# Weighted values of attention: one product of 128 columns for each block of keys in place of two of 64

## The chip, the core and the metric

The kernel runs on one core of a Trainium2 chip. TensorE (PE in the profile) multiplies matrices: it loads a stationary operand of up to 128 x 128 (weight loads, PEld in the profile) and moves a second operand through it into PSUM. VectorE (DVE), ScalarE (ACT) and GpSimd (POOL) work element by element, and SyncE (SP) issues most of the transfers. The metric is the device time of one execution in microseconds (us), lower is better.

## The reference

One layer of an encoder over 1024 tokens of width 1024: a SwiGLU feed-forward half step, then attention and an RWKV-7 scan side by side, an output projection, and a second feed-forward half step. Inputs and result are float32. The part that the change touches is the attention, 8 heads of 64 features with three banded patterns, each a softmax over the keys of its band, mixed by their denominators:

```python
DILATED_PATTERNS = ((128, 1), (512, 4), (2048, 16))

def _attention_group(za, cos, sin, out_g):
    ...
    for window, dilation in DILATED_PATTERNS:
        o, l = _dilated_attention(q, k, v, window, dilation)
        outs.append(o)
        lses.append(l)
    wts = jax.nn.softmax(jnp.stack(lses, axis=0), axis=0)
    o = jnp.sum(wts[..., None] * jnp.stack(outs, axis=0), axis=0)
    o = o * lax.rsqrt(jnp.mean(o * o, axis=-1, keepdims=True) + NORM_EPS)
    return o.reshape(B, S, ATT_WIDTH) * out_g

def _dilated_attention(q, k, v, window, dilation):
    ...
    s = jnp.where(valid, s, -jnp.inf)
    m = jnp.max(s, axis=-1, keepdims=True)
    p = jnp.exp(s - m)
    den = jnp.sum(p, axis=-1, keepdims=True)
    o = jnp.einsum('bhrnqk,bhrnkd->bhrnqd', p, vb.astype(jnp.float32)) / den
```

The product `p` by `v` in the last line is the one that is changed, for the first two patterns.

## The kernel before

The layer is worked off in stages: the first feed-forward half (about 0 to 640 us of the profiled execution), the projections (to 928), the attention with part of the RWKV projections beside it (928 to 1182), preparation and scan of the RWKV group with the output projection (to about 1600), the second feed-forward half.

In the attention the tokens are in 8 blocks of 128. The first two patterns are taken together in `near`: for a block of 128 queries, only the keys of at most 5 blocks count (two before, two after), 34 pairs of blocks for each head. `scores(t)` multiplies queries and keys of block `t` (L713, L714, in split single-pass float32), adds the band's bias and takes the maximum on VectorE (L715), and the exponential on ScalarE (L718). `turn(t)` transposes the 128 x 128 pieces of the exponentials on TensorE (L727), so that keys lie on partitions, and copies them out of PSUM (L728). `values(t)` multiplies them by the values and adds up over the key blocks in one PSUM tile `po` of 128 queries x 8 blocks x 64 features (L734). These run as a pipeline: in step `t` stand `scores(t)`, `turn(t - 1)` and `values(t - 2)`. When a head is done, `po` is scaled on VectorE (L758).

The third pattern, of stride 16, is worked in `far` for the next head between these steps (scores L655, transposes L666, values L673, on 64 x 64 parts of the array). After each head comes one stream of the RWKV projection (L523, 48 products of 512 columns; L599 and L609 belong to it). A scheduler orders all of it: it interleaves the products of L523 with those of the attention, so that each engine's list of instructions is fixed before the run, and TensorE works its list off in order. In the products of L655 and L673 and, before the change, of L734, the stationary operand has 64 columns and the result goes to partitions 0 to 63 or 64 to 127.

Of the kernel before, what the change touches and what calls it, by code (L numbers as in the profile page):

```python
# [31 lines left out]
def _ap(src, off, pat):  # L32
    return bass.AP(tensor=src.tensor, offset=src.offset + off, ap=pat)
# [130 lines left out]
class _Kernel:  # L164
# [529 lines left out]
    def near(self, psum, p, h, sq, kh, kl, v, far, between):  # L694

        nc, V, A, G, T = self.nc, self.nc.vector, self.nc.scalar, self.nc.gpsimd, self.nc.tensor
        hs = slice(h % 2 * 64, h % 2 * 64 + 64)
        nm, d = (p.tile([128, NT], F32, name=n, tag=n) for n in ("nm", "dn"))
        M = p.tile([128, 4 * NT], F32, name="M", tag="M")[:, :NT]
        cc = p.tile([128, 2, NT], F32, name="cc", tag="cc")  # L700
        po = psum.tile([128, NT, 64], F32, name="po", tag="o", bufs=1)
        S_, E_ = {}, {}
        keys = lambda t: (max(0, t - 2), min(NT, t + 3))

        def scores(t):
            k0, k1 = keys(t)
            n, qs = (k1 - k0) * 128, slice(t * 128, (t + 1) * 128)
            bias = self.bias12[:, (k0 - t + 2) * 128:(k0 - t + 2) * 128 + n]
            s = S_[t] = p.tile([128, 640], F32, name="sb", tag="sb")
            for c in range(0, n, 512):  # L710
                e = min(n, c + 512)
                ps = psum.tile([128, 512], F32, name="s12", tag="s", bufs=2)
                T.matmul(ps[:, :e - c], sq[:, qs], kh[:, k0 * 128 + c:k0 * 128 + e], start=True, stop=False)  # L713
                T.matmul(ps[:, :e - c], sq[:, qs], kl[:, k0 * 128 + c:k0 * 128 + e], start=False, stop=True)  # L714
                V.tensor_tensor_reduce(out=s[:, c:e], in0=ps[:, :e - c], in1=bias[:, c:e], scale=-1.0,  # L715
                                       scalar=nm[:, t:t + 1] if c else 3e38, op0=OP.add, op1=OP.min,
                                       accum_out=nm[:, t:t + 1])
            A.activation(s[:, :n], s[:, :n], AF.Exp, bias=nm[:, t:t + 1], scale=-1.0, accum_out=d[:, t:t + 1])  # L718

        def turn(t):  # L720
            n, s = (keys(t)[1] - keys(t)[0]) * 128, S_.pop(t)
            et = E_[t] = p.tile([128, 640], F32, name="e12", tag="e12")
            for c in range(0, n, 512):
                w = min(n - c, 512)
                pt = psum.tile([128, 512], F32, name="pt12", tag="t", bufs=2)
                for i in range(w // 128):
                    T.transpose(pt[:, i * 128:(i + 1) * 128], s[:, c + i * 128:c + (i + 1) * 128], self.ident)  # L727
                (V.tensor_copy if (t % 2 and not c) else A.copy)(et[:, c:c + w], pt[:, :w])  # L728

        def values(t):  # L730
            (k0, k1), et = keys(t), E_.pop(t)
            for i in range(k1 - k0):
                for c in range(0, 128, 64):
                    T.matmul(po[c:c + 64, t, :], et[:, i * 128 + c:i * 128 + c + 64], v[:, k0 + i, hs], start=(i == 0),  # L734
                             stop=(i == k1 - k0 - 1))

        for step in range(NT + 2):
            if step < NT:
                between(step)
                scores(step)  # L740
            if 1 <= step < NT + 1:
                turn(step - 1)
            if step >= 2:
                values(step - 2)
        f = far
        o = h % 2 * 64
        fd, fm, c12, c3 = f[:, :, o], f[:, :, 65], cc[:, 0], cc[:, 1]
        V.scalar_tensor_tensor(M, fm, -1.0, nm, op0=OP.mult, op1=OP.min)
        V.tensor_tensor(c12, M, nm, op=OP.subtract)
        V.tensor_tensor(c3, fm, M, op=OP.add)  # L750
        A.activation(cc, cc, AF.Exp)
        V.tensor_tensor(d, d, c12, op=OP.mult)
        V.tensor_tensor(M, fd, c3, op=OP.mult)
        V.tensor_tensor(d, d, M, op=OP.add)
        V.reciprocal(d, d)
        V.tensor_tensor(cc, cc, d[:, None, :].to_broadcast([128, 2, NT]), op=OP.mult)
        y = p.tile([128, NT, 64], F32, name="ya", tag="ya", bufs=1)
        V.tensor_tensor(y, po, c12[:, :, None].to_broadcast([128, NT, 64]), op=OP.mult)  # L758
        f3 = f[:, :, 1 - h % 2:65 - h % 2]
        G.tensor_tensor(f3, f3, c3[:, :, None].to_broadcast([128, NT, 64]), op=OP.mult)  # L760
        G.tensor_tensor(y, y, f3, op=OP.add)
        G.tensor_tensor(f3, y, y, op=OP.mult)
        V.tensor_reduce(out=self.ss_a[:, :, h], in_=f3, op=OP.add, axis=AX.X)
        self.nc.scalar.dma_start(_ap(self.ya_d, h * 64, [[512, 128], [128 * 512, NT], [1, 64]]), y)
# [710 lines left out]
```

## Time and profile before

| | |
|---|---|
| Median of 3 runs | 2297.95 us (2295.15 to 2307.57) |
| Profiled execution | span 2299.0 us; nothing is recorded around it |
| TensorE busy | 2198.8 us, 96% of the span |
| TensorE weight loads | 1781.8 us, 77% |
| VectorE, ScalarE, GpSimd busy | 77%, 45%, 23% |
| Products of L734 | 1088 records between 928.4 and 1179.2 us |

A record is one instruction on the chip. Matmuls are pipelined, so the length of one record (0.22 us for L734) is longer than the distance from its start to the start of the next, the pitch. In the views of groups, a line names the source line, the engine, the operation, the output and inputs, the stationary operand (128*64: 128 partitions, 64 columns) and the moving one (128x64), the number of records; then busy time in us and mean length in ns, then idle time of the engine just before them and what ended it. A row in order of time gives start and length in us.

### The profile page before, as it was taken

How to read it: one execution, taken by the hardware profiler on the slowest of the kernel's cores; microseconds unless marked ns; L12 is line 12 of the kernel's file. 1: busy time of each engine (PE TensorE's matmuls, PEld its weight loads, DVE VectorE, ACT ScalarE, POOL GpSimd, SP SyncE). 2: the span in 40 equal slices, each digit the busy share in tenths (PEclk: the TensorE clock that was granted, in tenths of full speed). 3: DMA queues.
4: the chain of work that ended last, by engine and by line, in shares of the span. 5: the costliest groups of instructions: out<-in, count | busy, mean ns of one | idle time of the engine just before them, and what ended most of it. 6: DMA issues, size and time to landing. Idle time of an engine off the chain costs nothing. (4 is left out here: it accounts for less than half of the span.)

```text
span 2299.0 us, 41391 instructions
## 1 busy us (share of the span) xinstructions
PE 2198.8 (96%) x15556; PEld 1781.8 (77%) x15556; DVE 1767.3 (77%) x2893; ACT 1023.6 (45%) x1925; POOL 537.0 (23%) x673
## 2 busy tenths in 40 slices
PE   7999999999999998999998899999799999999998
PEld 5788888878877676777776777776678888888887
DVE  7999999865676254677679678747999999997566
ACT  5322323354567411666654644455442323335453
POOL 2354443410000011222221111122024444441000
PEclk9999999999999999999999799999899999999999
DMA  5354545486662513654467746357445454548665
GB/s 151 124 183 151 170 147 173 164 266 193 193 225 78 212 72 105 186 147 144 131 178 184 211 136 167 107 173 257 155 135 174 150 174 151 170 152 282 194 194 187
DMA packets 346700, 387.74 MB, mean 169 GB/s; under 512 B 73474, under 2 KB 249346, under 8 KB 346500
## 3 DMA queue, kind: packets, MB, share of 16 engines
q1 hardware_dynamic: 294928, 271.71, 39.2%
q0 software_dynamic: 31216, 100.73, 11.6%
q10 hardware_dynamic: 20356, 12.66, 1.8%
q8 instruction: 122, 2.00, 0.4%
q14 instruction: 78, 0.64, 0.1%
HBM read 258.06 MB, written 126.94 MB: 167 GB/s over the span
## 5 line engine op out<-in xcount | busy, mean ns | idle before, releaser
L81 PE MATMUL gu<-xh,wh 128*128 128x512 f32 x704 | 277.3, 394 | 4.6 <-ACT wh L186 4.5
L186 ACT ACTIVATE wh<-raw 128x512 fp32r<-128x512 f32 (+1 forms) x273 | 168.3, 627 | 252.3 <-PE gu L81 95.7
L81 PE MATMUL gu<-xl,wh 128*128 128x512 f32 x704 | 276.0, 392 | 0.0
L81 PE MATMUL gu<-xh,wl 128*128 128x512 f32 x704 | 275.9, 392 | 0.0
L187 DVE TENSOR_TENSOR wl<-raw,wh 128x512 fp32r<-128x512 f32 (+1 forms) x273 | 270.4, 994 | 3.7 <-ACT wh L186 3.0
L421 PE MATMUL pd<-gl,gwh 128*128 128x512 f32 x616 | 240.6, 391 | 2.6 <-DVE gl L187 2.6
L421 PE MATMUL pd<-gh,gwh 128*128 128x512 f32 x616 | 239.8, 390 | 0.6 <-DVE row L86 0.6
L421 PE MATMUL pd<-gh,gwl 128*128 128x512 f32 x616 | 240.1, 390 | 0.2 <-DVE gwl L187 0.2
L86 DVE TENSOR_TENSOR row<-gu,row 128x512 f32<-128x512 f32 x308 | 206.6, 683 | 25.8 <-PE gu L81 23.5
L187 DVE TENSOR_TENSOR gwl<-graw,gwh 128x512 fp32r<-128x512 f32 (+2 forms) x187 | 118.8, 643 | 124.0 <-ACT gwh L186 122.3
L116 POOL DMA_DIRECT2D d_hid<-row x154 | 84.7, 551 | 546.0 <-DVE row L114 524.2
L186 ACT ACTIVATE gwh<-graw 128x512 fp32r<-128x512 f32 (+2 forms) x187 | 103.1, 554 | 187.2 <-PE pd L421 151.3
L81 PEld LDWEIGHTS gu<-xh,wh 128*128 128x128 f32 x704 | 133.4, 190 | 33.6 <-ACT wh L186 5.6
L81 PEld LDWEIGHTS gu<-xh,wl 128*128 128x128 f32 x704 | 133.2, 189 | 27.7 <-DVE wl L187 0.2
L81 PEld LDWEIGHTS gu<-xl,wh 128*128 128x128 f32 x704 | 133.3, 189 | 27.4
L421 PEld LDWEIGHTS pd<-gl,gwh 128*128 128x128 f32 x616 | 115.7, 188 | 27.8 <-DVE gl L187 3.9
L421 PEld LDWEIGHTS pd<-gh,gwh 128*128 128x128 f32 x616 | 115.6, 188 | 25.5 <-DVE row L86 1.0
L421 PEld LDWEIGHTS pd<-gh,gwl 128*128 128x128 f32 x616 | 115.7, 188 | 24.1 <-DVE gwl L187 0.6
L187 DVE TENSOR_TENSOR gl<-raw,gh 128x512 fp32r<-128x512 f32 x160 | 114.7, 728 | 22.9 <-ACT gh L186 22.6
L94 ACT ACTIVATE row<-row 128x512 f32<-128x512 f32 x44 | 27.8, 633 | 212.0 <-DVE row L86 212.0
L145 POOL TENSOR_TENSOR ws<-ws 128x512 f32<-128x512 f32 x88 | 114.6, 1303 | 1.2
L186 ACT ACTIVATE gh<-raw 128x512 fp32r<-128x512 f32 x160 | 98.1, 622 | 35.5 <-DMA raw<-in_ffn_w_down_dram 22.8
(364 smaller groups left out, 5238.2 us busy)
## 6 DMA issues: line engine op xcount, KB each, us to landing
d_hid<-row POOLq DMA_DIRECT2D x154, 256.0 KB, 2.5
graw<-d_hid SPq DMA_DIRECT2D x132, 256.0 KB, 2.9
raw<-in_ffn_w_gate_dram SPq DMA_DIRECT2D x88, 256.0 KB, 3.1
raw<-in_ffn_w_up_dram SPq DMA_DIRECT2D x88, 256.0 KB, 3.6
ws<-in_ffn_w_down_dram SPq DMA_DIRECT2D x88, 256.0 KB, 4.1
d_ws<-ws POOLq DMA_DIRECT2D x88, 256.0 KB, 2.3
raw<-d_ws SPq DMA_DIRECT2D x88, 256.0 KB, 2.8
raw<-in_ffn_w_down_dram SPq DMA_DIRECT2D x66, 256.0 KB, 3.6
```

Source lines behind the costliest of these rows:

```text
L81: self.K.nc.tensor.matmul(ps, a[:, k, :], b[:, k, :], start=(k == 0 and i == 0), stop=(k == 3 and i == 2))
L86: add = lambda o, x: V.tensor_tensor(o, ps, x, op=OP.add)
L94: A.activation(y[:, 0], y[:, 0], AF.Silu)
L116: put = lambda n, y: G.dma_start(self.hid[n - 1, j // 2], y)
L145: G.tensor_tensor(o, a, b, op=OP.subtract)
L186: self.nc.scalar.activation(h, src, AF.Copy)
L187: (eng or self.nc.vector).tensor_tensor(l, src, h, op=OP.subtract)
L421: T.matmul(ps[x], a[:, ts], b, start=(m == 0 and k == 0), stop=(m == NM - 1 and k == 2))
```

## The change

The two products of a key block, which each took 64 of the 128 queries as the stationary operand and wrote one half of the partitions, become one product with all 128 queries as the stationary operand. The moving operand, the 64 columns of the head's values, stays the same. The result is the same sum.

```diff
         def values(t):
             (k0, k1), et = keys(t), E_.pop(t)
             for i in range(k1 - k0):
-                for c in range(0, 128, 64):
-                    T.matmul(po[c:c + 64, t, :], et[:, i * 128 + c:i * 128 + c + 64], v[:, k0 + i, hs], start=(i == 0),
-                             stop=(i == k1 - k0 - 1))
+                T.matmul(po[:, t, :], et[:, i * 128:i * 128 + 128], v[:, k0 + i, hs], start=(i == 0),
+                         stop=(i == k1 - k0 - 1))
```

The line of the product moves from L734 to L733, and later lines by one. TensorE's list, at the end of the second head (query blocks 4 to 7), before; `pt` are transposes, `po` the products that are changed, `zr` the projections beside:

```order
L727 MATMUL pt_9355<-ident,sb 128x128 x4
L727 MATMUL pt_9361<-ident,sb 128x128
L734 MATMUL po<-vn,e_9328 64x64 x10
L523 MATMUL zr<-xh_5416,zh 128x512
L727 MATMUL pt_9381<-ident,sb 128x128 x4
L734 MATMUL po<-vn,e_9354 64x64 x10
L523 MATMUL zr<-xl_5417,zh 128x512
L523 MATMUL zr<-xh_5416,zl 128x512
```

The same place in the changed kernel:

```order
L733 MATMUL po<-vn,e_9214 128x64 x5
L714 MATMUL s_9251<-kl,sq 128x384
L523 MATMUL zr<-xl_5417,zh 128x512
L727 MATMUL pt_9236<-ident,sb 128x128 x4
L727 MATMUL pt_9242<-ident,sb 128x128
L523 MATMUL zr<-xh_5416,zl 128x512
L523 MATMUL zr<-xh_5416,zh 128x512
L523 MATMUL zr<-xl_5417,zh 128x512
L523 MATMUL zr<-xh_5416,zl 128x512
L727 MATMUL pt_9257<-ident,sb 128x128 x4
L733 MATMUL po<-vn,e_9235 128x64 x5
```

Ten products of 64 rows of output are five of 128; they stand in as many runs (74) as before, and the first block's run has moved ahead of the second score product of block 6. TensorE's list, where the far pattern's values (L673) come directly behind such a run, in the changed kernel:

```order
L727 MATMUL pt_9166<-ident,sb 128x128 x4
L727 MATMUL pt_9172<-ident,sb 128x128
L733 MATMUL po<-vn,e_9134 128x64 x5
L673 MATMUL po3t<-v_9048,e_9117 64x65 x8
L713 MATMUL s_9209<-kh,sq 128x128
```

There are five such places in the list before and five in the list of the changed kernel. On the other engines the instructions are the same in number and kind; their order differs in places, in the attention and in the scan behind it.

## Prediction

> **What bounds the kernel now.** I read the page first, then the busy time by stages, then what TensorE waits for in the stage of the change, then the instructions of that stage in order of time.
>
> ```profile
> span 2299.0 us, 41391 instructions
> 640.00:928.00 288.00, 274.83 (x1245) 207.98 (x1244) 147.39 (x208) 129.41 (x222) 21.09 (x31) 0.98 0.40 136
> 928.00:1182.00 254.00, 248.41 (x2454) 198.59 (x2453) 186.58 (x456) 163.69 (x377) 65.98 (x72) 0.99 0.49 147
> 1182.00:1520.00 338.00, 304.88 (x5319) 253.65 (x5319) 249.37 (x722) 164.09 (x296) 51.98 (x96) 0.88 0.63 174
> ```
>
> The last three lines are stages: length, then the busy time of PE, its weight loads, DVE, ACT and POOL, the granted clock, DMA. From 928 to 1182 us runs the banded attention, the only stage that the change touches. TensorE is busy 248.41 of its 254 us; DVE has 67 us free and ACT 90. What TensorE waits for there, by the view of waits:
>
> ```profile
> PE s L713 <- DVE nm L715: 2.2, 3, 1.0
> PE pt L727 <- ACT sb L718: 1.8, 3, 0.7
> PE s L713 <- DVE sb L659: 0.7, 1, 0.7
> PE po3s L673 <- DVE nm L715: 0.3, 1, 0.3
> PE pt L727 <- ACT e L728: 0.2, 1, 0.2
> ```
>
> That is 5.2 us in 254. The rest of the stage is TensorE's own order of work, so what the products of L734 gain or lose there moves the stage's end. What follows the stage stands behind it on the same queue: the first piece that the chain of waits holds is
>
> ```profile
> 1187.47 5.37 DMA d_v<-us
> ```
>
> a store of what the last products of L523 gave, and those stand behind the attention on TensorE. So I pass a change of the stage on one for one.
>
> **What the products of L734 cost now.** The view of the line:
>
> ```profile
> L734 PEld LDWEIGHTS po<-vn,e x1088: 132/138/228, 928.4 to 1179.1; 128*64 128x64 f32 x182
> L734 PE MATMUL po<-vn,e x1088: 221/222/369, 928.4 to 1179.2; 128*64 128x64 f32 x182
> ```
>
> The program has 8 heads x 34 key blocks x 2 halves = 544 products; the trace has 1088 records, so a product of this type (f32) is two loads and two passes. Their length (222 ns) is mostly pipeline; what counts is the pitch from start to start. Two places, in order of time (start, length, then the instruction), and the lengths of one record of L727 (least, median, most):
>
> ```profile
> 1004.32 0.73 PE L727 MATMUL pt<-ident,sb 128*128 128x128 f32 x5
> 1004.98 0.80 PE L734 MATMUL po<-vn,e 128*64 128x64 f32 x20
> 1005.71 0.50 PE L713 MATMUL s<-kh,sq 128*128 128x512 f32 x1
> 1006.05 0.39 PE L714 MATMUL s<-kl,sq 128*128 128x512 f32 x1
> ...
> 1021.25 0.40 PE L523 MATMUL zr<-xh,zl 128*128 128x512 f32 x1
> 1021.57 0.57 PE L734 MATMUL po<-vn,e 128*64 128x64 f32 x12
> 1022.07 0.50 PE L523 MATMUL zr<-xh,zh 128*128 128x512 f32 x1
> 1022.40 0.39 PE L523 MATMUL zr<-xl,zh 128*128 128x512 f32 x1
> 1022.64 0.40 PE L523 MATMUL zr<-xh,zl 128*128 128x512 f32 x1
> ...
> L727 PE MATMUL pt<-ident,sb x272: 269/273/418, 927.1 to 1177.7; 128*128 128x128 f32 x136
> ```
>
> Within the run of 20 the pitch is (0.80 - 0.222)/19 = 0.0305 us. Around it something else is paid. The last start of L727 is 1004.32 + 0.73 - 0.27 = 1004.78, and L714 starts at 1006.05, 1.27 later; without the run these would be one transpose (0.11, priced below) and one 512-column product (0.23, as 1022.40 to 1022.64), together 0.34. So the run costs 0.93, of which 20 x 0.0305 = 0.61 is its records and 0.32 is not. The run of 12 agrees: 1.15 from L523 to L523 less two pitches (0.46) is 0.69, less 0.37 is 0.32. It is a gap ahead of the run (1004.78 to 1004.98) and one behind it, and a first 512-column product that takes 0.34 in place of 0.23: the array goes from 128 stationary columns to two halves of 64 and back. The Trainium skill ("TensorEngine Tiling (Array Packing)", Key Properties) states that a change of the tiling mode drains TensorE; the 0.32 us is what that is here.
>
> TensorE's list of instructions has these products in 74 runs, before the change and after it. So they cost 74 x 0.32 = 23.7 us of switching and 1088 x 0.0305 = 33.2 us of records, **56.9 us** of the stage.
>
> **What they cost after.** It removes the switch and half of the records: 272 products, 544 records. Each now has 128 stationary columns and the same 64 moving ones. No row has just this form. The nearest are L599 (f32, 128 stationary columns, 2 moving), L727 (transposes, 128 moving) and L1039 (f32, 256 moving):
>
> ```profile
> 1024.25 1.98 PEld L599 LDWEIGHTS kn<-k_ones,ksq 128*128 128x128 f32 x16
> 1024.47 1.84 PE L599 MATMUL kn<-k_ones,ksq 128*128 128x2 f32 x16
> L599 PEld LDWEIGHTS kn<-k_ones,ksq 128*128 128x128 f32 x64 | 7.7, 192 | 0.3
> L599 PE MATMUL kn<-k_ones,ksq 128*128 128x2 f32 x64 | 7.4, 247 | 0.0
> ...
> 1582.13 1.03 PE L1039 MATMUL gate<-f_sg,g2w 128*128 128x256 f32 x4
> L1039 PE MATMUL gate<-f_sg,g2w x32: 379/380/484, 1540.9 to 1598.8; 128*128 128x256 f32 x32
> ```
>
> L599 moves almost nothing and still takes (1.84 - 0.247)/15 = 0.106 us a record, its loads (1.98 - 0.192)/15 = 0.119: this is the price of loading 128 columns, and the load is the limit. L727 gives (0.73 - 0.27)/4 = 0.115. L1039 gives (1.03 - 0.38)/3 = 0.217 for 256 moving columns, so 64 need about 0.054, and a load of 0.11 hides under a move of 0.217. I take the load as the limit and the move hidden under it: **0.111** us a record, 544 x 0.111 = **60.4 us**. The bounds: below, 0.061, what one half-array's record takes now (two halves share the 0.0305), as if a full load cost no more than half a load; above, 0.111 + 0.054 = 0.165, load and move one after the other. They give 33.2 and 89.8 us.
>
> The comparison is against the tiling's own gain: two halves load and multiply beside each other, so 128 columns are loaded in 2 x 0.0305 = 0.061 us where the full load takes 0.111. The Trainium skill's rule speaks against the change here (same page, Theoretical Speedup: with 64 or fewer stationary columns, up to 2 times). By it the records would go from 33.2 to at most 66.4 us; the rows give 60.4, so the sum would come out 6 us higher.
>
> By length of run: a run of 20 goes from 0.93 to 10 x 0.111 = 1.11 (+0.18), one of 12 from 0.69 to 0.67, one of 4 from 0.44 to 0.22. The break-even lies near 13 records; the mean run has 1088/74 = 14.7. So the sum is nearly even: 60.4 - 56.9 = **+3.5 us**.
>
> **What does not go away.** In 5 of the 74 runs the products of L673 follow, in the kernel before and in the changed one, and these keep an array of 64 x 64:
>
> ```profile
> 1001.18 0.76 PE L727 MATMUL pt<-ident,sb 128*128 128x128 f32 x5
> 1001.88 0.80 PE L734 MATMUL po<-vn,e 128*64 128x64 f32 x20
> 1002.61 0.27 PE L673 MATMUL po3t<-v,e 64*64 64x65 f32 x1
> ```
>
> From the last L727 (1001.67) to L673 are 0.94, less 0.11 and 0.61 leaves 0.22: one switch on the way in and none worth 0.32. After, the switch is paid between L734 and L673 instead. So 5 x (0.32 - 0.22) = 0.5 is less to save and 5 x 0.2 = 1.0 is paid anew: +1.5, in all +5.0 us. Against it stand the 5.2 us of waits: a middle block's products last 0.18 us longer, and the score and exponential work on DVE and ACT, which TensorE waits for in these places, gets that time. With about nine waits of 0.2 to 1.0 us, some of them behind such a block, I take 2 us back. **+3 us.** No wait is added: the products of a block still wait for the copy of L728, and the normalisation that reads all of po (L758) for the head's last product; 16 half-blocks or 8 whole ones make no difference to it.
>
> **The order.** The scheduler places the new products elsewhere by a few rows, and some work behind the stage too. Vector and scalar instructions are the same in number and kind, only in another order, so I cost this at nothing in the middle and in the range by what the clock shows:
>
> ```profile
> 1128.58 0.50 PE L713 MATMUL s<-kh,sq 128*128 128x512 f32 x1 [1.03 <-DVE nm L715]
> 1130.10 1.17 PE L727 MATMUL pt<-ident,sb 128*128 128x128 f32 x5 [0.57 <-ACT sb L718]
> ...
> 1201.89 0.63 PE L523 MATMUL zr<-xh,zh 128*128 128x512 f32 x1
> 1202.31 0.63 PE L523 MATMUL zr<-xl,zh 128*128 128x512 f32 x1
> ```
>
> After two waits at 1128 and 1130 five transposes take (1.17 - 0.42)/4 = 0.19 a record (0.42 is the longest of L727 in the row above) and not 0.115; at 1202 products of 512 columns come every 0.42 us and not 0.23. Between 1182 and 1520 the mean granted clock is 0.88, so 338 x 0.12 = 41 us of clock are lost to such stretches. The Trainium skill ("TensorE: Matmul & The Clock Gate", The HAM clock gate) says that idle windows of about 3.4 us halve the clock; the trace has the halving. Where another order shifts a wait, a stretch comes or goes; a quarter of those 41 us either way is 10 us.
>
> **Rivals.**
> - *Load and move in series* (0.165 a record): 89.8 - 56.9 + 1.5 = +34, median 2332. For it: no row shows 64 moving columns behind a full f32 load. Against: L1039 hides its load. It makes the kernel slower by over 0.5% from 0.111 + 8.5/544 = 0.127 us a record on. 0.05.
> - *A full load as cheap as a half one* (0.061): 33.2 - 56.9 + 1.5 = -22, median 2276. For it: half-array loads do come that fast. Against: all 64 loads of L599 and the loads of L727 are at 0.1 and more. The skill's clock-gate page (Weight-path perf modes) has a fast load for 128 columns that is not f32; these are f32, and no run here shows it. 0.05.
> - *The order decides*: waits and half-clock stretches move, the products hardly count. Up to 10 us either way, 2288 to 2311; I give it 0.20, of which faster by 0.5% takes 0.04, slower 0.06.
> - *The change does not reach the array*: excluded by the list of instructions, where the products write 128 rows.
>
> **How the numbers follow.** The profiled execution has a span of 2299.0 us, 1 us over the median of the three runs (2297.95), which range over 0.5%. 2298 + 3 = **2301 us**, with 0.70 for this forecast and 2293 to 2309 as its own range. A measurement of this kernel tells about 0.5% (11.5 us) from no change: below 2286.5 is faster, above 2309.4 slower. Faster: 0.05 cheap load, 0.04 order, 0.01 from the forecast's tail, 0.10. Slower: 0.05 series, 0.06 order, 0.03 tail (the sum's +5.0 with a poor order), 0.14. The rest, 0.76, is no change. The range for 8 in 10 takes in the order's shift on both sides and leaves the two prices of a load out: **2289 to 2314**.
>
> **What would show it.** In the profile after: 544 records of the new line with a pitch near 0.111 us in a run, at 128 x 128; no gap of 0.2 us between L727 and them; the 512-column product behind a run at 0.23 and not 0.34 to its successor; a stretch from the first to the last of these products within some 5 us of the 250.8 now. A pitch of 0.06 or of 0.16 proves the one or the other rival. If the stage's length is as said and the span is not, the order did it, and the stage from its end to 1520 shows where. I would be wrong in the working if the removed switches gave back much more or less than 0.32 us each.

## The result and the profile after

Median 2306.59 us of 9 runs (2301.06 to 2319.4) against 2299.28 of 9 (2293.64 to 2307.57). The ratio is 1.0041 with an interval of 1.0023 to 1.0059, so 5 to 14 us more; a second set of 12 runs gave 1.0034 (1.0018 to 1.0051). Both ratios lie inside the half per cent that the prediction called no change, the upper ends of their intervals a little above it; the median lies inside its range, and 4 to 7 us above what +3 us would have given.

The view of the new line, and the stages of the attention and of what follows (columns as in the prediction):

```profile
L733 PEld LDWEIGHTS po<-vn,e x544: 186/192/247, 928.1 to 1182.0; 128*128 128x128 f32 x182
L733 PE MATMUL po<-vn,e x544: 217/275/323, 928.2 to 1182.0; 128*128 128x64 f32 x182
...
928.00:1182.00 254.00, 249.30 (x1899) 215.86 (x1898) 183.95 (x454) 163.78 (x376) 63.76 (x70) 1.00 0.48 146
1182.00:1520.00 338.00, 292.70 (x5206) 244.19 (x5205) 249.11 (x725) 159.77 (x289) 53.67 (x98) 0.91 0.62 172
```

There are 544 records, and the first and last stand 253.8 us apart where it was 250.8: +3.0, the number forecast for the stage. The profiled execution has a span of 2301.9, +2.9 on the profiled one before. Another profiled execution of the same program has the same 253.8 and a span of 2309.4, and one of the kernel before has 2294.5: a single span tells little here, and the time is judged by the ratios.

Before the stage is believed, one run of the new products in order of time:

```profile
1047.64 0.62 PE L727 MATMUL pt<-ident,sb 128*128 128x128 f32 x4
1048.10 1.23 PE L733 MATMUL po<-vn,e 128*128 128x64 f32 x10
1049.13 0.48 PE L523 MATMUL zr<-xh,zh 128*128 128x512 f32 x1
1049.45 0.39 PE L523 MATMUL zr<-xl,zh 128*128 128x512 f32 x1
```

From the last start of L727 (1047.64 + 0.62 - 0.27 = 1047.99) to the second L523 (1049.45) are 1.46 us. The half products took 1.27 from their last L727 to L714 at the place shown in the prediction. The pitch within the run is (1.23 - 0.275)/9 = 0.106 us, and of all neighbours in runs the median is 0.112. The gap of 0.2 us ahead of the run is gone: L733 starts 0.11 after the last transpose.

What TensorE waits for behind the attention (1180 to 1550 us), the longest waits; before:

```profile
PE lp L858 <- DVE lm L860: 8.7, 8, 3.2
PE pa L916 <- ACT tt L912: 4.9, 2, 2.7
PE vt L640 <- DVE us L538: 4.2, 2, 3.7
```

and after:

```profile
PE lp L857 <- DVE lm L859: 12.6, 10, 4.1
PE pa L921 <- ACT am L918: 5.5, 2, 3.3
PE xu L962 <- issue: 5.2, 2, 4.4
```

Over the whole view these waits add up to 32.5 us before (34.3 in the second profile) and 43.8 after (42.6). No product there was changed.

### The profile page after: what moved, and what is told of

Same layout as the page of the kernel before. It is cut to its first block, busy times and chain, and to the rows that moved or that the text cites. A ratio compares the mean times of both kernels' runs of the same rounds, so it can differ in the third digit from the quotient of the medians.

```text
span 2301.9 us, 40307 instructions
## 1 busy us (share of the span) xinstructions
PE 2192.2 (95%) x15012; PEld 1792.6 (78%) x15012; DVE 1762.5 (77%) x2893; ACT 1024.0 (44%) x1925; POOL 538.1 (23%) x673
## 4 chain that ended last, share of the span: by engine, by line
PE 41%; DVE 7%; DMA 3%; issue 2%; ACT 2%; POOL 0%; SPq 0%; DVEq 0%; ACTq 0%; POOLq 0%
PE gu L81 18%; PE pd L421 9%; PE zr L523 3%; PE po L733 1%; DVE ttmp L893 1%; DVE Ti L895 1%; PE po L1079 1%; PE lp L857 1%; PE pt L727 1%; PE st L958 1%; DVE lm L859 1%; PE y L958 1%; DMA wor<-in_w_out_dram 1%; DMA X<-d_x 0%; PE s L713 0%
## 5 line engine op out<-in xcount | busy, mean ns | idle before, releaser
L81 PE MATMUL gu<-xl,wh 128*128 128x512 f32 x704 | 275.6, 391 | 0.0
```

The lines of the kernel that those rows point to most:

```text
L81: self.K.nc.tensor.matmul(ps, a[:, k, :], b[:, k, :], start=(k == 0 and i == 0), stop=(k == 3 and i == 2))
```

## Experiments

Two theories had to be told apart. The first is that of the prediction: the products alone make the difference, at prices of 0.0305 us a record and 0.32 us a switch before against 0.111 us a record after. The second: the order in which the scheduler put everything else makes it.

### The same two kernels again

No edit.

> The kernel before once more, as a second set of times with the mean granted clock of each execution. Theory of the products (records of 0.0305 us in half-arrays, 0.32 us a switch): the stretch from the first to the last product of L734 is again 250.8 us within 0.5. Rival (the order of the work behind the attention and its half-clock stretches make the difference): executions of this kernel scatter too, time falls with the clock, and the scatter lies between 1182 and 1520 us. Ratio to before 1.000 within 0.003.

> The changed kernel once more. Theory of the products: the stretch of L733 is again 253.8 us within 0.5, so the change itself is worth +3 us (ratio 1.0013). Rival: three of nine executions lay near 2317 us at a lower clock (0.968 to 0.973) and six near 2303 (0.974 to 0.980); if that group comes back in a like share and the kernel before has none, the ratio is again 1.003 to 1.005 while the stretch of L733 is unchanged, and the rest of the difference lies in the stages behind it.

Measured: the kernel before against itself 0.9999 (0.9982 to 1.0017), the changed kernel 1.0034 (1.0018 to 1.0051). The stretches of the products were 250.7 and 253.8 us, as in the first profiles. The changed kernel's 12 runs lay between 2300 and 2314 in one spread, without the two groups that the first nine suggested. So the changed kernel is slower by about 8 us, of which about 3 are in the stretch from its first value product to its last.

### Every product twice

```diff
-            for i in range(k1 - k0):
+            for i in list(range(k1 - k0)) * 2:
```

in the kernel before (`twice_halves`) and in the changed one (`twice_whole`). The second pass starts the sum again.

> The kernel before with every product of 64 columns made twice (the second pass starts the sum again, so the result is that of one). 1088 records more in runs of double length, the number of switches nearly unchanged (70 runs). Theory of the products: 1088 x 0.0305 = +33 us in the stage and, passed on one for one, in the time: 2332, ratio 1.014. Rival 1 (a fixed cost by record of 0.06 or more, so that the mean of 56.9/1088 = 0.052 is the record's own): +57 to +65 us. Rival 2 (the stage has slack that the rows do not show): under +20 us.

> The changed kernel with every product of 128 columns made twice. 544 records more, each of them a load of 128 columns. Theory of the products: 544 x 0.111 = +60 us over the changed kernel, +63 over the kernel before: about 2363, ratio 1.028. Rival 2 (slack): under +40 over the changed kernel. Together with the run of doubled halves: the whole product's records cost 27 us more than the halves' records, and the switches that went were worth 24.

Measured: 2331.26 us, ratio 1.0136 (1.0109 to 1.0164), and 2361.34 us, ratio 1.0266 (1.0236 to 1.0295). The records, the last projection and the last scan product of that form, doubled halves and then doubled whole products:

```profile
L734 PE MATMUL po<-vn,e x2176: 222/222/271, 929.7 to 1200.5; 128*64 128x64 f32 x198
L523 PE MATMUL zr<-xh,zl x176: 387/393/776, 919.9 to 1271.0; 128*128 128x512 f32 x176
L974 PE MATMUL xu<-xs,tt x512: 216/218/365, 1303.1 to 1569.7; 64*64 64x64 f32 x171
```

```profile
L733 PE MATMUL po<-vn,e x1088: 217/275/323, 929.2 to 1236.4; 128*128 128x64 f32 x182
L523 PE MATMUL zr<-xh,zl x176: 387/390/775, 919.3 to 1307.8; 128*128 128x512 f32 x176
L973 PE MATMUL xu<-xs,tt x512: 216/218/365, 1341.3 to 1602.0; 64*64 64x64 f32 x171
```

1088 records more in half-arrays cost 33 us (2331.26 - 2298.17), so 0.030 each; 544 more at full width cost 54 us over the changed kernel's 2307.74, so 0.099 each, with a mean pitch of 0.109 in the runs. The first hits the expectation and the second is 6 us short of its 60; the totals of rival 2 (slack: under 20 and under 40 us) are not seen.

That the first total is 33 is in part luck. The scheduler laid out these two programs anew, and the profiles put the time elsewhere than expected. From the first value product to the last L523 the doubled halves take 341.3 us, only 24 more than the 317.4 of the kernel before, with TensorE's waits there down from 5.2 to 2.1 us; the doubled whole products take 378.6, 59 more than the 319.3 of the changed kernel, or 0.109 for each record. About 6 us of each total come behind the last scan product, and between the last L523 and that product the doubled whole products save 9. The prices of a record therefore rest on the pitch in the runs, a mean of 0.0305 us here for halves and of 0.109 for whole products. That added time in the stage reaches the end is better seen below, in the halves one after the other, where the order is held.

### Whole and half products, each in the other's order

Here the lists of all engines were held in a given order by same-engine ordering edges, from a table that was read off the other kernel's built program:

```diff
+        for a, b in zip(at, at[1:]):
+            tc.add_manual_dep(mine[int(b)], mine[int(a)].name, info, reason="order")
...
     with tile.TileContext(nc) as tc:
         _Kernel(tc, io, out).run()
+        _arrange(tc, nc)
```

> The products of 128 columns, but every engine's list of instructions held in the order of the kernel before (each pair of half products replaced by the whole one at the place of its first). Theory of the products alone: +3 us over the kernel before (stretch of the products 253 to 254 us), behind the attention nothing changes, so the waits of TensorE from 1180 to 1550 us are those of the kernel before (32 to 34 us): ratio 1.001 to 1.002. Theory that the order behind the attention costs the rest (4 to 6 us of the 8): this kernel loses that rest, 2300 to 2302. Rival (the whole products themselves cost 8 us, also by way of the clock): ratio 1.003 to 1.004 as for the changed kernel.

> The reverse: the half products of the kernel before, every engine's list held in the order of the changed kernel. Theory of the order: the 42 to 44 us of waits of TensorE from 1180 to 1550 us come back, and the time is the kernel before plus 4 to 6 us, ratio 1.002 to 1.003, although no product is changed. Rival: ratio 1.000 within 0.001.

Measured: whole products in the old order 2311.96 us, ratio 1.0061 (1.0038 to 1.0083); half products in the new order 2301.5 us, ratio 1.0013 (0.9999 to 1.0027), which decides neither for the 1.002 to 1.003 expected of the order nor for the rival's 1.000. The rows of the products, of the last projection L523 and of the last scan product of that form, for half products in the old order (the kernel before, whose first row stands in the prediction):

```profile
L523 PE MATMUL zr<-xh,zl x176: 387/394/794, 919.2 to 1245.8; 128*128 128x512 f32 x176
L974 PE MATMUL xu<-xs,tt x512: 215/218/365, 1285.5 to 1544.4; 64*64 64x64 f32 x171
```

half products in the new order:

```profile
L734 PE MATMUL po<-vn,e x1088: 222/222/271, 930.4 to 1179.6; 128*64 128x64 f32 x182
L523 PE MATMUL zr<-xh,zl x176: 387/393/775, 922.1 to 1244.3; 128*128 128x512 f32 x176
L974 PE MATMUL xu<-xs,tt x512: 213/218/365, 1280.3 to 1545.6; 64*64 64x64 f32 x171
```

whole products in the new order (the changed kernel):

```profile
L523 PE MATMUL zr<-xh,zl x176: 387/394/776, 918.4 to 1247.6; 128*128 128x512 f32 x176
L973 PE MATMUL xu<-xs,tt x512: 213/218/365, 1281.6 to 1548.6; 64*64 64x64 f32 x171
```

whole products in the old order:

```profile
L733 PE MATMUL po<-vn,e x544: 217/275/323, 929.9 to 1185.3; 128*128 128x64 f32 x182
L523 PE MATMUL zr<-xh,zl x176: 387/393/793, 920.3 to 1253.9; 128*128 128x512 f32 x176
L973 PE MATMUL xu<-xs,tt x512: 216/218/365, 1291.3 to 1551.2; 64*64 64x64 f32 x171
```

The differences of these, the first value product to the last L523, and from there to the last scan product, in us (in brackets the second profile of the same program):

| | attention | behind it |
|---|---|---|
| halves, old order | 317.4 (317.4) | 298.6 (294.9) |
| halves, new order | 313.9 | 301.3 |
| whole, old order | 324.0 | 297.3 |
| whole, new order | 319.4 (319.1) | 301.0 (305.0) |

Read down, the product costs 6.6 us in the old order and 5.4 in the new one (319.3 less 313.9), all in the attention. Read across, the new order saves 3.5 and 4.7 us in the attention and costs about 4.5 (301.3 less the mean 296.8) and 5.7 us behind it, nearly even in sum. The second column is the weaker one, since two profiles of one program differ there by 4 us. Both theories hold a part: the products cost more than the +3, and the reordering hid some of it in the attention and gave that back behind. The waits of TensorE from 1180 to 1550 us grow with the order when the products stay half products (from 32 to 34 us to 40.5), but not with the order alone: with whole products in the old order they were 38.6, not the 32 to 34 expected.

The expectation for whole products in the old order (2300 to 2302) failed, and so did the 1.001 to 1.002 of the products alone; the rival's 1.003 to 1.004 lies at the lower end of the interval. Its profiled span is 2306.8, +10 on the mean of the two profiles before; the table accounts for about 7 of it. Its six timed runs lie higher still, at 14 us by the ratio (9 to 19), and why is not settled. No run held a kernel in its own order, so what the holding itself costs was not measured; `runs_of_2` below, held in the same way, is at 0.9995. By the ratios the whole products thus cost about 14 us in the old order and some 5 in the new one (1.0034 less 1.0013), where the table has 6.6 and 5.4.

Two pairs of kernels here have equal lists but for the products, so their starts can be set against each other, instruction by instruction. The lag is how much later an instruction starts with whole products than with half ones. Each line is its mean growth over one run of products, and over how many runs; runs that other products cut apart in one of the two have no line:

```
records in a run    whole - half, old order    whole - half, new order
20 -> 10            +0.22 us (24)              +0.22 us (26)
16 -> 8             +0.06 us (12)              +0.08 us (17)
12 -> 6              0.00 us (14)               0.00 us (17)
 8 -> 4             none                       -0.11 us (9)
 4 -> 2             one run                    -0.22 us (5)
sum over all runs   +4.9 us                    +4.8 us
```

The sums depend on the instruction behind a run at which the lag is read: at the second or third they come to 4 to 5 us.

### Longer runs: two and four blocks together

```diff
-            et = E_[t] = p.tile([128, 640], F32, name="e12", tag="e12")
+            et = E_[t] = p.tile([128, 640], F32, name="e12", tag="e12", bufs=3)
...
-            if step >= 2:
-                values(step - 2)
+            if step >= 2 and (step - 1) % 2 == 0:
+                with self.tc.tile_critical():
+                    for t in range(step - 1 - 2, step - 1):
+                        values(t)
```

`fours` puts four blocks in a section and has five buffers.

> Half products as before, but the values of two query blocks are made in one uninterrupted run (three buffers in place of two for the transposed exponentials): 32 runs in place of 74, records unchanged. Theory of the switch (0.32 us each): 42 x 0.32 = 13 us less on TensorE, so 2285 (ratio 0.994) if the order behind does not matter, 2280 to 2291 with it. Rival (a switch costs nothing of its own, the gaps around a run are waits that would come anyway): ratio 1.000 within 0.002. A risk on the other side: a run waits for two blocks' exponentials, and TensorE with it.

> As pairs, with four query blocks in a run (five buffers): 16 runs, 58 x 0.32 = 18.6 us less switching than before, so 2280 (ratio 0.992), 2275 to 2287 with the order behind. If the switch costs what the rows say, the step from pairs to fours is half of the first step (5 us). Rival: no step, or a loss from waiting for four blocks.

Measured: 2412.71 us, ratio 1.0496 (1.0471 to 1.052), and 2387.15 us, ratio 1.0377 (1.0352 to 1.0403). What TensorE waits for from 900 to 1400 us in `pairs`:

```profile
PE po L734 <- DMA zraw<-in_w_in_dram: 14.6, 6, 4.1
PE po L734 <- DMA d_n<-n: 7.0, 3, 3.4
PE po L734 <- DMA kp<-d_kt: 6.6, 2, 3.5
```

The value products need none of these transfers. By this view the uninterrupted section waits for what the other queues have under way (in `fours` likewise), so the two runs say nothing of the switch. They were made again with the order held instead, with no section: the list of the kernel before, in which the products of the two (or four) blocks follow each other at the place of the last block's first.

> Half products in the order of the kernel before on every engine, only that the runs of two query blocks' values are moved behind each other on TensorE (to the place of the second block's first product; three buffers in place of two for the transposed exponentials): 32 runs in place of 74, 1088 records as before. Theory of the switch (0.32 us each): 42 x 0.32 = 13 us less from the first to the last product (250.7 to 237), and 2285 in all if it passes on, ratio 0.994. Rival (what stands around a run are waits that come anyway): stretch 250 and ratio 1.000. Against the run named pairs: there the runs waited for transfers and other engines (over 60 us); here nothing new is waited for, so if the time is again over 2350, a longer run itself does harm.

> As before with four query blocks in a run (five buffers): 16 runs. Theory of the switch: 58 x 0.32 = 18.6 us less, stretch 232, about 2280, ratio 0.992; the step from 32 to 16 runs is 5 us. Rival: no gain, or a loss where the later values hold up the copies of the exponentials and the end of a head.

> Whole products in the order of the kernel before, with the runs of two blocks put together in the same way. Here there is no switch to save (but for the runs ahead of L673), so theory of the switch: stretch 254 to 256 as with whole products in that order (255.5), ratio 1.003 to 1.006. Rival (putting runs together gains for another reason): the stretch falls by as much as with half products, some 13 us.

Measured: 2299.94 us, ratio 0.9995 (0.9975 to 1.0016), for 32 runs; 2310.57 us, 1.0042 (1.0022 to 1.0061), for 16; 2327.66 us, 1.0097 (1.006 to 1.0134), for whole products in pairs. None does what its theory of the switch expected, and `runs_of_2` comes out at the numbers of its rival, by which the gaps around a run are waits that would come anyway. The rows say otherwise. In `runs_of_2` a pair of blocks of ten products each, in order of time:

```profile
1011.97 0.66 PE L727 MATMUL pt<-ident,sb 128*128 128x128 f32 x4 [0.21 <-ACT e L728]
1012.56 1.39 PE L734 MATMUL po<-vn,e 128*64 128x64 f32 x40
1013.87 0.50 PE L523 MATMUL zr<-xl,zh 128*128 128x512 f32 x1
1014.21 0.39 PE L523 MATMUL zr<-xh,zl 128*128 128x512 f32 x1
```

From the last transpose (1011.97 + 0.66 - 0.27 = 1012.36) to the second L523 are 1.85 us; less 0.34 for a transpose and a projection, and 40 x 0.0305 = 1.22, this leaves 0.29 for the one switch of two blocks. So here the second switch is saved. But TensorE waits in its place, here in `runs_of_2` between 925 and 1184 us:

```profile
PE s L713 <- DVE nm L715: 3.8, 4, 1.5
PE pt L727 <- ACT sb L718: 3.7, 6, 0.7
PE pt L727 <- ACT e L728: 1.4, 5, 0.4
PE s L713 <- DVE sb L659: 1.4, 1, 1.4
PE pt L727 <- ACT kh L688: 1.1, 2, 0.5
```

With the smaller ones these are 14.8 us against 5.2, and the stretch of the products is 250.2 against 250.7. Outside its waits the stretch thus fell from 245.5 to 235.4 us, by about 10 and not by the 13 expected of 42 switches. With four blocks the waits are 22.7 us.

The work of a block goes through score product, maximum (L715), exponential (L718), transpose and copy (L728), and TensorE now waits for this chain. That it does so because it is through its own list sooner is not shown, and the pairs of whole products speak against it. They have hardly a switch to save, and their longest waits between 925 and 1207 us are nearly the same, again 14.8 us in all:

```profile
PE s L713 <- DVE nm L715: 4.0, 5, 1.5
PE pt L727 <- ACT sb L718: 3.8, 6, 0.7
PE pt L727 <- ACT e L728: 1.4, 5, 0.4
PE s L713 <- DVE sb L659: 1.4, 1, 1.4
PE pt L727 <- ACT kh L688: 1.1, 2, 0.5
```

So the waits come with the products that were moved to a later place; that there they no longer fill the time of the chain is the likely reason. For whole products in pairs the stretch grew from 255.5 to 275.6 us: 14.8 us of waits in place of 5.6, and the granted clock over the stage is 0.97 where it was 1.00, which is some 8 us of its 278. That these two make up the growth is only argued; which of the two causes the other was not tried.

### The halves one after the other

```diff
-            for i in range(k1 - k0):
-                for c in range(0, 128, 64):
+            for c in range(0, 128, 64):
+                for i in range(k1 - k0):
```

with every engine's list in the order of the kernel before.

> Half products, order of the kernel before on every engine; only within a run all products of the lower half come ahead of those of the upper half, so that neighbours use the same half of the array. Theory that the pitch of 0.0305 us is two halves working beside each other: a record now takes 0.055 to 0.061, so 1088 x 0.0275 = +30 us (+25 to +33), ratio 1.011 to 1.014. Rival (a record of 64 columns takes 0.03 us by itself): no change.

Measured: 2327.57 us, ratio 1.0103 (1.0073 to 1.0133). A run of 20 records:

```profile
1009.16 1.20 PE L734 MATMUL po<-vn,e 128*64 128x64 f32 x20
```

The pitch is (1.20 - 0.222)/19 = 0.051 us, and over all runs the mean goes from 0.033 to 0.054. So the 0.0305 of the kernel before comes of neighbours in different halves of the array, which overlap. The Trainium skill ("TensorEngine Tiling (Array Packing)", Theoretical Speedup) gives up to 2 times for this; here 0.051 against 0.0305 in a run of 20 is 1.7, and 0.054 against 0.033 over all runs is 1.6. The price is 24 us by the ratio (17 to 31), a little under the 25 to 33 expected; the stretch of the products grew by 20.6 (271.3 less 250.7). With the order held, this is the plainest sign that added time in the stage is passed on.

## Why the prediction was right, and where it was off

*TensorE bounds the stage, and added time is passed on.* This held. With the order held, the halves one after the other added 20.6 us to the stretch and 24 to the whole; the doubled products added 33 and 54 us to the whole, though not where it was expected. That saved time is passed on as well is not shown: in the pairs of blocks new waits took the place of the saved switches, and they came with the new places of the products.

*0.0305 us a record, 0.32 us a switch.* The record held: the mean pitch in the doubled kernel is 0.0305, and it is 0.051 to 0.054 where the halves do not alternate. The switch held at the place shown, with 0.29 us for the one switch of a run of 40. Over the whole stage 42 fewer runs saved about 10 us outside the waits, 0.24 each.

*0.111 us for a whole record.* This held, with a mean pitch of 0.109 in the doubled kernel, a median of 0.112 in the changed one. The move adds nothing that shows beside the load, and both rivals on the price fell by the rows: neither 0.061 nor 0.165 is seen.

*By length of run.* +0.18 for 20 records, -0.02 for 12 and -0.22 for 4 were worked out; +0.22, 0.00 and -0.22 were measured. The sum over the runs, +3.5 and +1.5 for the places that keep their switch, is +4.9 and +4.8 in the two pairs of equal order. One sign of it was wrongly named: the 512-column product behind a run still has 0.32 us to its successor and not 0.23. It starts only 0.08 us behind the last product of the run, while its own load still runs, and with 0.112 us for each of ten records and 0.34 for a transpose and a projection the 1.46 us are accounted for.

*"I take 2 us back."* This step failed. In the same order the waits of the attention are 5.6 us with whole products and 5.2 with halves: nothing was given back, and the attention grew by another 1 to 2 us outside the runs. So the products' own term is +5 to +7 by the profiles and not +3.

*"I cost this at nothing in the middle."* The order's two effects nearly cancel, -3.5 to -4.7 us in the attention and +4.5 to +5.7 behind it, and the stretch of +3.0 that met the forecast is in truth the products' +4.6 (halves in the new order 249.2, whole 253.8) less what the new order saved there. So the stage came out as forecast by luck, and the ratios of 1.0034 and 1.0041 hold the part behind it too. The sum of the parts, 5 to 7 for the products and 0 to 3 for the order, lies within the 5 to 14 us of the ratios. Whether anything is left over cannot be told at this resolution for the changed kernel; for whole products in the old order something is, since 14 us (9 to 19) stand against 7, and its cause stays open.

## What to carry to other kernels

A product with few moving columns, here 64, can be priced by the load of its stationary operand: in this kernel two half-width products that alternate between the halves of the array load as much in 0.06 us as one full-width product in 0.11, and the halves pay for that with a switch of 0.2 to 0.3 us at each run. So the length of the uninterrupted run decides (here the break-even is at 12 records, three key blocks), and it is read from the list of instructions, not from the code. And where a scheduler lays out the program, a change is to be judged with the order held, since here the order alone moved single stages by 3.5 to 5.7 us, nearly as much as the products did. A time that comes out as forecast does not show that its terms were right: in the stage of the products two of them were off here and nearly cancelled.

## What the runs showed of the hardware

From the last transpose of the second feed-forward half's input to the end, 609.7 us passed in nearly all of these kernels (609.7 to 610.0 in 14 profiles); so what scatters from execution to execution lies ahead of it. Two profiles of the kernel before differ by 4.5 us, of which 3.7 between about 1245 and 1545 us; two of the changed kernel by 7.5, of which 4.0 there. The granted clock in that stretch was 0.88 to 0.91.

With an uninterrupted section around the value products of two blocks, TensorE's waits between 925 and 1280 us add up to 70 us where they were 5 in the attention before, most of them for transfers and engines that those products do not use.
